# One gate of the modulation, computed in the second layer's token selection instead of in the first mixer

## The chip, the cores and the metric

One core of a Trainium2 chip runs the kernel. The metric is the device time of one execution in microseconds (us); lower is better. Five engines work beside one another, each through its own list of instructions in order: PE (TensorE, matrix products), DVE (VectorE), ACT (ScalarE), POOL (GpSimd) and SP (SyncE, here only an issuer of transfers). Sixteen DMA engines move data; they are fed by a hardware queue (transfers that SP issues) and a software queue (transfers that POOL issues).

## What is computed

A transformer of two layers for 512 image tokens ("l") and 256 context tokens ("c"), width 1024, in float32. In each layer a modulation vector of six parts is made from the condition `c`:

```python
mod_l = (silu_c @ w_mod[l] + b_mod[l])[:, None, :]
sh1, sc1, g1, sh2, sc2, g2 = jnp.split(mod_l, 6, axis=-1)
h_l = modulate(rms_norm(x, norm1_g[l]), sh1, sc1)
x = x + g1 * token_mixer(h_l, ...)
h_l = modulate(rms_norm(x, norm2_g[l]), sh2, sc2)
x = x + g2 * expert_choice_ffn(h_l, ...)
```

Each part has 1024 columns. `expert_choice_ffn` lets each of 16 experts choose its 64 best tokens (a softmax over experts, then a top-64 over tokens), runs a gated FFN of width 1024 on them, and adds the result back, times the gate `g2`. Scale 2 (`sc2`) is thus first needed where the router of a layer is prepared, gate 2 (`g2`) only where the first pair of experts has finished.

## The kernel before, in words

The program runs layer 0 and then layer 1, each in four stages: the **mixer** (input projections, retention, attention), the **output projection**, the **selection** (normalisation, router, top-64, slots) and the **experts** in eight pairs. Experts of both layers stream their weights (2 MB a load, SP's queue) through a ring of slots in on-chip memory; a load starts when the slot's last reader on PE is done.

*Modulation.* `mod_gen` (L185 to L209) makes blocks of 2048 columns. For each of eight row blocks of `w_mod` (128 rows each) it loads 2 x 512 KB on SP's queue (L197, tiles `wm`), multiplies with the 32 columns of `cT` in four matmuls that stand side by side in four column groups of PE (L201, `ps_mod`), and adds the result to `modt` on DVE (L203). One such visit is one `yield`. Block 2 holds scale 2 and gate 2. At its end the block is written to a scratch tensor in device memory (L207), and `mod_cols` (L240 to L259) transposes it with four PE transposes (L244, `ps_mc`) into the columns `A2`. The visits are woven into the first layer's projections: `m0` (L1572) is a chain of generators, `weave` takes a step of it for every so many steps of the projections and of attention, and what is left is drained when attention ends. The first layer thus computes all three blocks of the second layer as well.

*The second layer's gate.* `gates2` (L1068) reads gate 2 back, spread over 128 partitions, by one transfer on SP's queue (L264, `mod_row`); it is called in `passes` (L1748) before the last part of the selection.

*The second layer's selection.* `passes` ends with an iterator of the steps that are left (`R.fin`: the rest of `Norm2.half`, `softmax`, `keep`, `top`, `slots_l`), and the code after it opens the last three ring slots, issues their loads (`ring.load(N2)`, SP L1495) and drains the steps (L1801). On PE that is: transposes of x (L911), router products (L923), `ps_r<-qsum` (L942), four products that turn the affinities (L988, L990), then nothing until the eight rounds of top-8 on DVE are done (L996 to L999), then the products of `slots_l` (L1012, L1026). The gather of the first pair follows at once (L1111, DVE L1115, PE L1123 `ps_x`), and then its gate matrix (L1133 `ps_g`). POOL has the additions of the residual (L891) and one memset (L983) there.

The order on each engine is the order in which the tile framework's scheduler put the instructions; for the experts' stage PE's order is that of the code.

## Time and profile before

| | |
|---|---|
| median of 3 runs | 1892.11 us (1891.56 to 1894.91) |
| the profiled execution | 1889.7 us |
| its span, first to last instruction | 1887.9 us |
| mean granted clock of PE | 0.976 of 2.4 GHz |
| PE busy | 1770.4 us (94%) |
| hardware queue (SP) | 511.24 MB |
| software queue (POOL) | 15.26 MB |

Times in the rows are microseconds from the span's start. The first mixer lies at about 30 to 412, the first layer's experts end at about 1050, the second mixer at about 1330, its selection lies at 1377 to 1404, and the second layer's experts fill the time from there to 1875. A line number is that of the kernel before (L201) unless the text says "of the change". The records of PE show two rows for one float32 product, so eight records are four matmuls.

### The profile page before, as it was taken

How to read it: one execution, taken by the hardware profiler on the slowest of the kernel's cores; microseconds unless marked ns; L12 is line 12 of the kernel's file. 1: busy time of each engine (PE TensorE's matmuls, PEld its weight loads, DVE VectorE, ACT ScalarE, POOL GpSimd, SP SyncE). 2: the span in 40 equal slices, each digit the busy share in tenths (PEclk: the TensorE clock that was granted, in tenths of full speed). 3: DMA queues.
4: the chain of work that ended last, by engine and by line, in shares of the span. 5: the costliest groups of instructions: out<-in, count | busy, mean ns of one | idle time of the engine just before them, and what ended most of it. 6: DMA issues, size and time to landing. Idle time of an engine off the chain costs nothing. (4 is left out here: it accounts for less than half of the span.)

```text
span 1887.9 us, 30047 instructions
## 1 busy us (share of the span) xinstructions
PE 1770.4 (94%) x12581; PEld 1018.5 (54%) x12581; DVE 655.8 (35%) x1671; ACT 479.8 (25%) x960; POOL 329.9 (17%) x341
## 2 busy tenths in 40 slices
PE   5899999999899999999999789899959999999995
PEld 2788877767533333333333688877745444534442
DVE  5645435673621001110001755446341122221224
ACT  3435434353411001010000446454331000000001
POOL 3323123333201011011001333322410000000001
PEclk9999999999899999999999899999979999999998
DMA  8454354257789999999998411111747999999995
GB/s 278 155 191 157 106 202 151 90 186 279 300 340 408 414 401 401 423 400 399 395 412 325 169 43 37 57 34 38 297 185 291 420 430 429 429 429 428 431 428 206
DMA packets 88919, 528.42 MB, mean 280 GB/s; under 512 B 9352, under 2 KB 31932, under 8 KB 64720
## 3 DMA queue, kind: packets, MB, share of 16 engines
q1 hardware_dynamic: 83040, 511.24, 68.0%
q0 software_dynamic: 5744, 15.26, 2.9%
q8 instruction: 99, 1.62, 0.3%
q14 instruction: 36, 0.29, 0.0%
HBM read 510.41 MB, written 16.06 MB: 279 GB/s over the span
## 5 line engine op out<-in xcount | busy, mean ns | idle before, releaser
L1133 PE MATMUL ps_g<-ring,xTl 128*32 128x512 f32 (+1 forms) x1472 | 238.0, 596 | 4.2 <-DMA ring<-in_w_gate_dram 3.0
L1133 PE MATMUL ps_u<-ring,xTl 128*32 128x512 f32 (+1 forms) x1536 | 233.1, 592 | 3.1 <-DMA ring<-in_w_up_dram 2.4
L1133 PE MATMUL ps_d<-ring,aT 128*32 128x512 f32 (+1 forms) x1536 | 234.6, 593 | 0.3 <-ACT sil L1241 0.3
L1270 ACT ACTIVATE aT<-ps_t 128x512 f32<-128x512 f32 x16 | 9.6, 598 | 619.0 <-PE ps_t L1266 578.1
L354 PE MATMUL acc<-wH,hHl 128*128 128x256 f32 x512 | 153.8, 301 | 2.7 <-ACT hHl L343 1.2
L1133 PEld LDWEIGHTS ps_g<-ring,xTl 128*32 128x32 f32 (+1 forms) x1472 | 72.7, 121 | 154.1 <-issue 137.5
L1133 PEld LDWEIGHTS ps_u<-ring,xTl 128*32 128x32 f32 (+1 forms) x1536 | 69.9, 119 | 153.1 <-issue 146.0
L355 PE MATMUL acc<-wH,hLl 128*128 128x256 f32 x512 | 147.0, 287 | 3.5 <-DVE hLl L344 3.4
L356 PE MATMUL acc<-wL,hHl 128*128 128x256 f32 x512 | 147.1, 287 | 1.1 <-DVE wL L276 1.1
L1133 PEld LDWEIGHTS ps_d<-ring,aT 128*32 128x32 f32 (+1 forms) x1536 | 70.4, 119 | 142.5 <-issue 136.7
L354 PEld LDWEIGHTS acc<-wH,hHl 128*128 128x128 f32 x512 | 99.7, 195 | 30.3 <-issue 23.7
L276 POOL TENSOR_TENSOR wL<-wraw,wH 128x512 fp32r<-128x512 f32 x44 | 57.5, 1308 | 275.0 <-ACT wH L275 263.8
L355 PEld LDWEIGHTS acc<-wH,hLl 128*128 128x128 f32 x512 | 99.8, 195 | 4.4 <-DVE hLl L344 4.4
L356 PEld LDWEIGHTS acc<-wL,hHl 128*128 128x128 f32 x512 | 99.8, 195 | 4.0 <-DVE wL L276 2.4
L1268 DVE COPY aT<-ps_t 128x512 f32<-128x512 f32 x16 | 11.1, 692 | 253.2 <-PE ps_t L1266 253.2
L1249 DVE TENSOR_TENSOR sil<-ps_u,sil 128x512 f32<-128x512 f32 x32 | 22.1, 692 | 220.8 <-PE ps_u L1133 220.8
L1185 POOL TENSOR_TENSOR x<-z,xTl 128x512 f32<-128x512 f32 x3 | 5.1, 1717 | 493.4 <-DVE x L1187 493.4
L678 DVE TENSOR_REDUCE mc<-ps_s 128x1 f32<-128x513 f32 (+2 forms) x80 | 55.2, 690 | 83.3 <-PE ps_s L675 52.1
L275 ACT ACTIVATE wH<-wraw 128x512 fp32r<-128x512 f32 x88 | 55.1, 629 | 95.6 <-PE acc L355 44.9
L680 ACT ACTIVATE P<-ps_s,mc 128x513 f32<-128x513 f32 (+2 forms) x80 | 55.1, 689 | 94.5 <-DVE mc L678 94.5
L1123 PE MATMUL ps_x<-OT,xn 128*128 128x128 f32 x512 | 67.0, 297 | 8.1 <-DVE OT L1115 8.1
L1123 PEld LDWEIGHTS ps_x<-OT,xn 128*128 128x128 f32 x512 | 65.3, 210 | 10.0 <-DVE OT L1115 8.5
(491 smaller groups left out, 3172.0 us busy)
## 6 DMA issues: line engine op xcount, KB each, us to landing
ring<-in_w_up_dram SPq DMA_DIRECT2D x62, 2048.0 KB, 16.6
ring<-in_w_gate_dram SPq DMA_DIRECT2D x61, 2048.0 KB, 13.3
ring<-in_w_down_dram SPq DMA_DIRECT2D x61, 2048.0 KB, 17.0
wm<-in_w_mod_dram SPq DMA_DIRECT2D x96, 512.0 KB, 4.6
wraw<-in_w_in_dram SPq DMA_DIRECT2D x44, 512.0 KB, 3.9
wraw_o<-in_w_out_dram SPq DMA_DIRECT2D x24, 512.0 KB, 4.1
ring<-in_w_gate_dram SPq DMA_DIRECT2D x12, 512.0 KB, 4.8
ring<-in_w_down_dram SPq DMA_DIRECT2D x12, 512.0 KB, 15.6
```

Of the source, the lines that this page charges most:

```text
L275: ACT.activation(H, src, AF.Copy)
L276: sub_eng().tensor_sub(L, src, f32(H))
L354: PE.matmul(ps, aH, bH, start=start, stop=False)
L355: PE.matmul(ps, aL, bH, start=False, stop=False)
L356: PE.matmul(ps, aH, bL, start=False, stop=stop)
L678: DVE.tensor_reduce(mc[:, 0:1], sc, AX.X, OP.max, negate=True)
L680: ACT.activation(P[:, :nk + 1], sc, AF.Exp, bias=mc[:, 0:1], accum_out=mc[:, 1:2])
L1123: PE.matmul(ps[:, j], R.xn[:, t, c0:c0 + 128], OT[:, t], start=(t == 0), stop=(t == 3))
L1133: PE.matmul(G[h][c:c + n], lhs[:, k, c:c + n], W[e][:, j, 512 * h:512 * h + 512], start=(k == 0), stop=(k == KC - 1), tile_position=(0, c))
L1249: DVE.tensor_mul(sil[p][:, hs], U[h], sil[p][:, hs])
L1268: DVE.tensor_copy(aT[p][:, 4 * h:4 * h + 4], ps)
L1270: ACT.activation(aT[p][:, 4 * h:4 * h + 4], ps, AF.Copy)
```

## The change

Block 2 of the second layer is no longer made by `mod_gen`. Its two halves go separate ways.

- **Scale 2** is made in the first mixer by `mod_a2`, at the end of the same chain: only columns 4096 to 5119, so 8 loads of 512 KB instead of 16, and four visits instead of eight, each with two row blocks in the four column groups. At its end come the same four transposes, a copy, an addition of the two partial sums, and the two instructions that make `A2`.
- **Gate 2** is made in the second layer's selection by `mod_g2`: 16 loads of 256 KB on POOL's queue into three slots (`wg2`), one matmul of 32 x 512 after each, into one PSUM bank, two DVE additions of 1 x 512, two writes to the scratch tensor on SP's queue, and then `gates2`, which has moved behind all this.

```diff
+NG2 = 3
...
+    def mod_a2(wp, pp):
...
+        for k in range(0, KC, 2):
+            ps = pp.tile([128, 512], F32, name="ps_mod", tag="t", bufs=4)
+            for i in range(2):
+                w = wp.tile([128, 2, 512], F32, name="wm", tag="wraw", bufs=NW)
+                SP.dma_start(w, w_mod[1, 128 * (k + i):128 * (k + i) + 128, 4096:5120].rearrange("p (q n) -> p q n", q=2))
+                for q in range(2):
+                    g = 32 * (2 * i + q)
+                    PE.matmul(ps[g:g + 32], cT[:, k + i, :], w[:, q, :], start=True, stop=True, tile_position=(0, g))
+            DVE.tensor_add(m, m, ps)
+            if k < KC - 2:
+                yield
...
+    def mod_g2(wp, pp):
+
+        m = wp.tile([64, 512], F32, name="modg")
+        for q in range(2):
+            POOL.dma_start(m[32 * q:32 * q + 1], b_mod[1:2, 5120 + 512 * q:5632 + 512 * q])
+        ps = pp.tile([128, 512], F32, name="ps_g2", tag="acc", bufs=4)
+        for k in range(KC):
+            for q in range(2):
+                w = wp.tile([128, 512], F32, name="wg2", tag="wg2", bufs=NG2)
+                POOL.dma_start(w, w_mod[1, 128 * k:128 * k + 128, 5120 + 512 * q:5632 + 512 * q])
+                PE.matmul(ps[32 * q:32 * q + 32], cT[:, k, :], w, start=k == 0, stop=k == KC - 1,
+                          tile_position=(0, 32 * q))
+            yield
+        for q in range(2):
+            o = slice(32 * q, 32 * q + 1)
+            DVE.tensor_add(m[o], m[o], ps[o])
+            SP.dma_start(mod_d[1][2][0:1, 1024 + 512 * q:1536 + 512 * q], m[o])
...
-                    m0 = chain(mod_gen(0, wq, pp, range(1, 3)), router_cols(0, streams, pp, R), mod_gen(1, wq, pp, range(0, 3)))
+                    m0 = chain(mod_gen(0, wq, pp, range(1, 3)), router_cols(0, streams, pp, R), mod_gen(1, wq, pp, range(0, 2)), mod_a2(wq, pp))
...
-                    gates2(l, ra[0], R, two)
                     if two:
+                        gates2(l, ra[0], R, two)
...
+                if not two:
+                    with ExitStack() as s4:
+                        g2 = mod_g2(s4.enter_context(tc.tile_pool(name="g2w", bufs=1, side="right")), pp)
+                        for i, _ in enumerate(R.fin):
+                            if i >= 8:
+                                next(g2, None)
+                        drain(g2)
+                        gates2(l, ra[0], R, two)
                 drain(R.fin)
```

What the scheduler makes of it, at three places. In the listings a name like `wg_12184` is a tile with its number; lines of the change are those of the diff's new file (L280 is the matmul of `mod_g2`, L279 its load, L274 its load of `b_mod`; L942 has become L990, L990 and L988 have become L1038 and L1036, L1012 is L1060, L1026 is L1074, L1111 is L1159).

PE in the second layer's selection, before, from the router's last products to the gather:

```order
4363 L923 MATMUL ps_lg<-hsc,wrAl 32x128 x8
4364 L942 MATMUL ps_r<-qsum,lgs 128x16 x4
4365 L990 MATMUL ps_r<-ident,aff_l 16x128 x2
4366 L988 MATMUL ps_r<-ident,aff_l 16x128 x2
4367 L1012 MATMUL ps_r<-val,ident 16x64
4368 L1012 MATMUL ps_r<-fi,ident 16x64
4369 L1026 MATMUL ps_r<-ident,tok_l 64x8 x2
4371 L1111 MATMUL ps_t<-tok_l,ident 128x64 x2
```

The same place now (left out are the matmuls that only repeat, the fifth to the eleventh of sixteen):

```order
4355 L971 MATMUL ps_lg<-hsc,wrAl 32x128 x8
4356 L280 MATMUL ps_g_12183<-wg_12184,cT 32x512
4357 L990 MATMUL ps_r<-qsum,lgs 128x16 x4
4358 L280 MATMUL ps_g_12183<-wg_12187,cT 32x512
4359 L280 MATMUL ps_g_12183<-wg_12190,cT 32x512
4360 L1038 MATMUL ps_r<-ident,aff_l 16x128
4361 L280 MATMUL ps_g_12183<-wg_12193,cT 32x512
4362 L1038 MATMUL ps_r<-ident,aff_l 16x128
4363 L1036 MATMUL ps_r<-ident,aff_l 16x128 x2
4371 L280 MATMUL ps_g_12183<-wg_12246,cT 32x512
4372 L1060 MATMUL ps_r<-val,ident 16x64
4379 L280 MATMUL ps_g_12183<-wg_12264,cT 32x512
```

The sixteen matmuls of the gate stand between the selection's own: one before the router's sums, three before the affinities are turned, twelve before the result of the top-64, all sixteen before the gather.

POOL from the last additions of the residual on, now (before, its two additions L891 stood next to each other, and nothing but the memset followed):

```order
240 L939 TENSOR_TENSOR x<-x,ty 128x512
241 L274 DMA modg<-in_b_mod_dram 1x16x32 x2
242 L939 TENSOR_TENSOR x<-x,ty 128x512
243 L279 DMA wg_12184<-in_w_mod_dram 128x512
244 L279 DMA wg_12187<-in_w_mod_dram 128x512
245 L279 DMA wg_12190<-in_w_mod_dram 128x512
246 L1031 MEMSET affT 48x256
247 L279 DMA wg_12193<-in_w_mod_dram 128x512
```

Three loads are issued behind the last addition; the fourth, and each one after it, waits for the matmul that frees its slot.

PE at the end of the first mixer, before (attention's score products left out between the two groups):

```order
1956 L711 MATMUL ps_o<-PT,avl 64x256 x2
1957 L201 MATMUL ps_mod<-wm,cT 32x512 x4
1964 L711 MATMUL ps_o<-PT,avl 64x256 x4
1965 L698 MATMUL ps_t<-ident,P 128x128 x4
1966 L201 MATMUL ps_mod<-wm,cT 32x512 x4
1967 L698 MATMUL ps_t<-ident,P 128x128 x2
1968 L244 MATMUL ps_mc<-ident,modt 128x128
1969 L698 MATMUL ps_t<-ident,P 128x128 x2
1970 L244 MATMUL ps_mc<-ident,modt 128x128 x3
1971 L698 MATMUL ps_t<-ident,P 128x128 x8
```

And now:

```order
1955 L759 MATMUL ps_o<-PT,avl 64x256 x5
1962 L759 MATMUL ps_o<-PT,avl 64x256
1963 L746 MATMUL ps_t<-ident,P 128x128 x16
1964 L759 MATMUL ps_o<-PT,avc 64x256 x4
```

The last four visits are gone, two of them from this place and two from some 70 rows ahead of it, and the four transposes have moved some 90 rows ahead.

## Rows read from the trace of the kernel before

**Rows 1.** Stretches: us, busy time (instructions) by engine, granted clock, DMA share, GB/s.
```profile
360.00:400.00 40.00, 39.41 (x272) 28.83 (x272) 28.15 (x91) 15.52 (x29) 13.69 (x15) 1.00 0.36 119
400.00:412.00 12.00, 11.36 (x90) 6.77 (x88) 6.40 (x16) 7.97 (x17) 2.40 (x3) 1.00 0.50 176
1460.00:1860.00 400.00, 387.33 (x1940) 178.69 (x1938) 87.17 (x161) 31.00 (x60) 0.00 (x0) 0.99 1.00 426
```

**Rows 2.** Timeline of PE, end of the first mixer: start, length, engine, line, operation.
```profile
388.06 1.06 PE L201 MATMUL ps_mod<-wm,cT 128*32 128x512 f32 x8
389.06 0.50 PE L354 MATMUL acc<-hHl,wH 128*128 128x512 f32 x1
...
406.12 1.07 PE L201 MATMUL ps_mod<-wm,cT 128*32 128x512 f32 x8
...
408.07 0.36 PE L244 MATMUL ps_mc<-ident,modt 128*128 128x128 f32 x1 [0.51 <-ACT P L685]
```

**Rows 3.** Timeline of PE, the second layer's selection and its first gather.
```profile
1383.72 1.06 PE L942 MATMUL ps_r<-qsum,lgs 128*128 128x16 f32 x8 [0.72 <-ACT lgs L939]
1388.12 0.59 PE L990 MATMUL ps_r<-ident,aff_l 128*16 128x128 f32 x2 [3.34 <-DVE aff_l L951]
...
1400.06 0.37 PE L1012 MATMUL ps_r<-val,ident 16*16 16x64 f32 x2 [9.75 <-DVE val L996]
...
1403.34 1.08 PE L1111 MATMUL ps_t<-tok_l,ident 16*128 16x64 f32 x4 [0.43 <-DVE slot_l L1037]
1404.96 5.81 PE L1123 MATMUL ps_x<-OT,xn 128*128 128x128 f32 x32 [0.54 <-DVE OT L1115]
1411.37 7.09 PE L1133 MATMUL ps_g<-ring,xTl 128*64 128x512 f32 x32 [0.60 <-ACT xTl L1089]
1418.39 3.84 PE L1123 MATMUL ps_x<-OT,xn 128*128 128x128 f32 x32
```

**Rows 4.** Timeline of DVE: the first of the eight rounds of top-8.
```profile
1390.80 0.42 DVE L996 MAX8 val<-affT 48x8 f32<-48x256 f32 x1
```

**Rows 5.** Stretches (columns as in rows 1) around the selection, and one early.
```profile
32.00:36.00 4.00, 2.45 (x12) 1.09 (x11) 4.00 (x6) 2.84 (x6) 2.65 (x3) 1.00 0.92 306
1392.00:1396.00 4.00, 0.00 (x0) 0.00 (x0) 3.90 (x17) 1.26 (x1) 0.00 (x0) 0.50 0.37 156
1404.00:1408.00 4.00, 3.46 (x16) 3.31 (x17) 1.13 (x4) 0.00 (x0) 0.00 (x0) 0.50 1.02 344
```

**Rows 6.** Timeline of POOL and of SP's transfers, start of the selection.
```profile
1376.40 3.44 POOL L891 TENSOR_TENSOR x<-x,ty 128x512 f32<-128x512 f32 x2 [3.02 <-DVE ty L890]
1377.03 0.80 SPq L1495 DMA_DIRECT2D ring<-in_w_up_dram  x2
```

**Rows 7.** DMA queues, 1380 to 1393: packets, MB, share of the 16 DMA engines.
```profile
q1 hardware_dynamic: 370, 5.54, 99.7%
```

**Rows 8.** Line L192, b_mod loads of 8 KB on POOL's queue: ns of an issue, landing.
```profile
L192 POOL DMA_DIRECT2D modt<-in_b_mod_dram x10: 549/564/573, 31.3 to 260.8; - x10
...
DMA to landing us min/median/max: 2.1/3.6/5.8
```

**Rows 9.** Tile xe, 1000 to 1040: three loads of 1 MB on POOL's queue, beside the ring.
```profile
DMA to landing us min/median/max: 11.4/12.3/13.1
```

**Rows 10.** DMA queues, 1021 to 1022: those loads (rows of 4 KB) beside the ring.
```profile
q1 hardware_dynamic: 20, 0.33, 76.4%
q0 software_dynamic: 23, 0.09, 22.9%
```

**Rows 11.** DMA queues, 616 to 617: POOL's scatter (rows of 2 KB) beside the ring.
```profile
q1 hardware_dynamic: 19, 0.31, 74.1%
q0 software_dynamic: 18, 0.03, 18.8%
```

**Rows 12.** Timeline of SP's transfers: the first ring loads that need a slot freed by the experts.
```profile
1413.33 16.88 SPq L1501 DMA_DIRECT2D ring<-in_w_gate_dram  x12
```

**Rows 13.** Tile g, five broadcasts of a gate (512 KB, L264): time to landing.
```profile
DMA to landing us min/median/max: 7.1/10.7/14.3
```

More of the change, by code (lines that the diff above doesn't have):

```diff
@@ L238, in mod_half @@
             DVE.scalar_tensor_tensor(A1[0][r][:, cs], tmp[:, 1, :, r], 1.0, n1col[0][:, cs], op0=OP.add, op1=OP.mult)
+        yield
+    def mod_a2(wp, pp):
+        m = wp.tile([128, 512], F32, name="modt", tag="modt", bufs=2)
+        POOL.memset(m, 0.0)
+        for r in range(2):
+            POOL.dma_start(m[r:64:32], b_mod[1, 4096:5120].rearrange("(q n) -> q n", q=2))
+        for k in range(0, KC, 2):
[9 more added lines that the diff above has]
+                yield
+        ps = pp.tile([128, 4, 4, 32], F32, name="ps_mc", tag="t", bufs=4)
+        for j in range(4):
+            PE.transpose(ps[:, j].rearrange("p q r -> p (q r)"), m[:, j::4], ident)
+        tmp = m[:, 0:32].rearrange("p (q s r) -> p q s r", q=4, r=2)
+        DVE.tensor_copy(tmp, ps[:, :, :, 0:2].rearrange("p s q r -> p q s r"))
+        DVE.tensor_tensor(tmp[:, 0:2], tmp[:, 0:2], tmp[:, 2:4], OP.add)
+        for r in range(2):
+            DVE.scalar_tensor_tensor(A2[1][r].rearrange("p (q s) -> p q s", q=2), tmp[:, 0:2, :, r], 1.0,
+                                     n2col[1].rearrange("p (q s) -> p q s", q=2), op0=OP.add, op1=OP.mult)
+        yield
@@ new lines, in mod_g2 @@
+    def mod_g2(wp, pp):
[9 more added lines that the diff above has]
+                          tile_position=(0, 32 * q))
+            yield
+        for q in range(2):
+            o = slice(32 * q, 32 * q + 1)
+            DVE.tensor_add(m[o], m[o], ps[o])
+            SP.dma_start(mod_d[1][2][0:1, 1024 + 512 * q:1536 + 512 * q], m[o])
```

## The prediction

> **What bounds the kernel now.** I read the page's forty slices first, to find the stages, then stretches of a few microseconds in the two stages that the change touches, then their timelines. In the first mixer PE sets the pace: from 360 to 400 it is busy 39.4 of 40 us at the full 2.4 GHz clock [rows 1], so work taken off PE there comes off the time. The last 12 us are less tight (11.36 of 12). In the experts the transfers set the pace: from 1460 to 1860 the DMA engines are busy 1.00 of the time at 426 GB/s, PE 387 of 400 [rows 1]. The stream that fills this time is limited by slots: its first transfer that waits for the experts starts at 1413.33 [rows 12], 2 us after the first gate matmul at 1411.37 [rows 3]. What makes the selection longer therefore moves the start of the stream, and the end, by the same amount. The selection is a chain: router sums on PE at 1383.72, affinities turned from 1388.12, the top-64 on DVE from 1390.80, its result on PE at 1400.06, the gather's first matmul (L1111) at 1403.34 [rows 3, 4]. PE is idle in most of it, and that is the room which the change uses. But PE takes its instructions in order, so a matmul that waits for its load holds up those behind it.
>
> **What the mixer gains.** Eight visits of four matmuls become four. A visit starts at 388.06 and the next product at 389.06 [rows 2]: 1.00 us. The four that go are the last four, 388.06 to 406.12. Three of them stand among work that PE does without a gap: 3.0 us. The fourth and the four transposes (408.07) stand where PE waits for ACT's softmax (0.51 us, released by ACT P) [rows 2], so ACT is late next and I count 0.3 us of a possible 1.5. Half of the 16 loads of 512 KB on SP go too; the DMA share there is 0.36 [rows 1], so that is worth nothing. Four DVE additions go, and a few small ones come, under PE's cover. Together -3.3 us, bounds -2 and -4.5.
>
> **What the selection loses.** The first load of gate 2 is issued on POOL behind the last residual addition, which ends at 1376.40 + 3.44 = 1379.84 [rows 6], and behind the two loads of b_mod, 0.56 us each [rows 8]: 1380.9. The second addition itself is moved back by those 1.1 us, into a gap in front of the last transposes, where PE was still at the products ahead of them; I count nothing.
>
> How long does such a load take? Alone, an 8 KB load on this queue lands in 2.1 us at best [rows 8]; 256 KB at 426 GB/s add 0.6: 2.7 us, the lower bound. But three ring loads are issued from 1377.03 [rows 6] and fill the DMA engines until about 1393.5 (share 0.997 up to 1393, 0.37 from 1392 to 1396) [rows 5, 7]. Where both queues have work, the rows show piece against piece: in one microsecond 20 ring pieces of 16 KB and 23 of 4 KB from POOL's queue [rows 10], and 19 against 18 where POOL moves rows of 2 KB [rows 11]. A load of this change is 128 rows of 2 KB, 8 for each of 16 engines. A ring piece takes 16 KB x 16 / 426 GB/s = 0.62 us of its engine, so eight turns of 0.62 + 0.08 are 5.6 us, and the first load lands near 1380.9 + 2.1 + 5.6 = 1388.6. As an upper bound, 1 MB loads beside the ring took 11.4 us and more [rows 9]; with half as many pieces an engine, 7.7 us fits between.
>
> The Trainium skill ("DMA: Bandwidth & Descriptors", section Queues, rings and completion order) states that an engine turns between queues by whole packets, typically of 9 to 17 descriptors. By that rule the eight rows of a load would go in one turn and the first would land near 1384; rows 10 and 11 speak for turns of single pieces, and I go by them. The rule's outcome is the first rival.
>
> Now the chain. A matmul of 32 x 512 is two records; the gate rows show 32 records in 7.09 us, two side by side [rows 3], so one alone takes 7.09 / 16 x 2 = 0.88 us, at half clock 1.77. PE has been waiting since 1383 and its clock falls to 0.50 when it idles, as in rows 5. So the first gate matmul ends at 1390.4, and the router sums start there instead of at 1383.72: +6.7. The affinities take 4.4 us more [rows 3], to 1394.8; the second and third load, which PE needs before it turns them, land 5.6 us later (1394.2) and soon after, when the ring is through; the fourth, issued when the first slot came free at 1390.4, lands about 1396.2 and stands between the two transposes. With their matmuls at half clock the second transpose comes near 1399, and the top-64 starts 2.4 us behind it, at 1401 instead of 1390.8: +10. It lasts 9.7 us, to 1411.
>
> The remaining twelve loads run three at a time. A slot's round is 0.6 issue, 2.7 to land and 0.9 for the matmul: 4.2 us, or 1.4 a load. The fifth lands near 1400, the sixteenth at 1400 + 11 x 1.4 = 1415.4, and its matmul ends at 1416.3. L1111 stands behind it: +13 against 1403.34. If the issue lies within the 2.7 the round is 3.6 us, and it is +11. I take **+12**; the bounds are +1 (each load in 2.7 us from the start) and +17 (the clock stays at half, 5.1 us a round: 1400 + 18.7 + 1.8).
>
> **What else moves.** PE is then no longer idle ahead of the gather. Before, its clock stood at 0.50 from 1392 to 1396 and still from 1404 to 1408, and the gather's 32 records took 5.81 us; the next 32 took 3.84 [rows 3, 5]. Early in the program PE kept the full clock while busy 2.45 of 4 us [rows 5], and the gate's matmuls make it about that busy. So -2.0 us, bounds 0 and -2.5. The two DVE additions of one row stand ahead of the gather's one-hot (L1115), which waits for L1111 anyway: +0.4, bounds 0 and 1.4. On SP the two writes and the broadcast of the gate now stand behind the selection, ahead of the slot-bound ring loads. The additions (1 us) and a write of a few KB (2.1 to 5.8 us, as the loads of rows 8) after the sixteenth matmul let SP go on 3 to 7 us later, and those ring loads are due 10 us after L1111 [rows 3, 12], 8 with the faster gather: covered. The broadcast lands in 7.1 to 14.3 us [rows 13], and its first reader, the end of the first pair, comes some 70 us on. If that cover went, SP's delay would add to the stream one to one.
>
> **Sum.** -3.3 + 12 + 0.4 - 2.0 = **+7.1 us**. The profiled execution took 1889.7 us (span 1887.9), which gives 1896.8; the median shown is 2.4 above it, so against the median I forecast **1899.2 us**. About 0.2% (3.8 us) is what a measurement can tell from no change.
>
> **Rivals.**
> - *The loads come early.* A load's eight pieces pass the ring pieces in one turn; the first lands by 1384, and rounds of 3.6 to 4.2 us bring the sixteenth by 1404 to 1405. The selection loses 1 to 2 us, the mixer and the gather give 5.3: -3 to -5, 1887 to 1889, not slower than before. It decides at a landing of about 3.3 us: with rounds much longer than that the sixteen no longer fit into 1381 to 1403. For it: from 1394 on the DMA engines are free. Against: rows 10 and 11. Chance 0.22. The Trainium skill's rule above speaks for this one.
> - *Two rows a turn.* Pieces of 2 KB go in pairs, as 4 KB rows did in rows 10: the first load lands at 1385.7, the top-64 starts 6 us late, the end of the loads is at +7: net +2, 1894. Chance 0.16.
> - *PE stays at half clock* through the loads: selection +17, gather no faster: +14, 1906. For it: 0.50 at PE idle [rows 5]. Against: at 1.77 us a matmul, with a round of 5.1 us for three, PE would hardly idle. Chance 0.13.
> - *The change doesn't lighten the mixer*: the four visits filled gaps that the softmax leaves, and nothing comes off; +10, 1902. Against: 39.4 of 40 us busy. Chance 0.05.
>
> **Chances.** The forecast has the remaining 0.44, with its own range of +3.5 to +10. Faster by over 0.2% is most of the first rival and a little of the second: 0.20. Within 0.2%: the rest of these and the forecast's lower edge: 0.21. Slower: 0.59. The range is to leave out the edge of the first rival and of the cold one: 1887.5 to 1906.
>
> **What would show it.** Right: in the changed profile PE's idle time ahead of the router sums and of the transposes ends with the landing of `wg2`; the first `wg2` lands 6 us or more after its issue, the later ones in about 3; the sixteenth matmul ends after 1410 on a clock set back by 3 us; the gather's 32 records take below 4.5 us. The mixer ends 3 us earlier. Wrong: `wg2` loads land in 3 us from the first on, the top-64 starts within 2 us of before, or the gather is reached before the mixer's gain is spent.

## The result, and the profile after

The change takes 1908.59 us (median of 4 runs, 1908.42 to 1917.79) against 1891.84 us (median of 4 runs of the kernel before on the same chip): a ratio of 1.0104, 95% interval 1.0083 to 1.0125. It is slower, by more than twice the forecast, and above the range. The profiled execution took 1908.42 us, its span 1906.6.

The timeline of PE in the second layer's selection, in the kernel of the change (start, length, line, operation, count; in brackets the idle time before it and what ended it). L280 is the gate's matmul, L990 the router's sums, L1038 and L1036 the turned affinities, L1060 the result of the top-64, L1159 the first product on the chosen slots, L1171 the gather, L1181 the experts' first product; the last product of the output projection starts at 1371.47:

```profile
1371.47 0.39 PE L404 MATMUL acc<-wL,mHl 128*128 128x512 f32 x1
...
1377.25 0.43 PE L971 MATMUL ps_lg<-hsc,wrAl 128*32 128x128 f32 x8 [0.28 <-DVE hsc L962]
1384.78 1.91 PE L280 MATMUL ps_g<-wg,cT 128*32 128x512 f32 x2 [7.10 <-DMA wg<-in_w_mod_dram]
1386.62 1.89 PE L990 MATMUL ps_r<-qsum,lgs 128*128 128x16 f32 x8
1388.44 1.92 PE L280 MATMUL ps_g<-wg,cT 128*32 128x512 f32 x2
1391.67 1.91 PE L280 MATMUL ps_g<-wg,cT 128*32 128x512 f32 x2 [1.31 <-DMA wg<-in_w_mod_dram]
1393.51 0.38 PE L1038 MATMUL ps_r<-ident,aff_l 128*16 128x128 f32 x1
1393.83 1.92 PE L280 MATMUL ps_g<-wg,cT 128*32 128x512 f32 x2
...
1396.63 0.39 PE L1036 MATMUL ps_r<-ident,aff_l 128*16 128x128 f32 x1 [0.57 <-DVE affT L1039]
...
1408.60 0.28 PE L1060 MATMUL ps_r<-val,ident 16*16 16x64 f32 x2
...
1413.73 1.04 PE L280 MATMUL ps_g<-wg,cT 128*32 128x512 f32 x2
1416.35 0.62 PE L1159 MATMUL ps_t<-tok_l,ident 16*128 16x64 f32 x4 [1.57 <-DVE modg L285]
1421.49 5.15 PE L1171 MATMUL ps_x<-OT,xn 128*128 128x128 f32 x32 [4.52 <-DVE OT L1163]
1427.24 7.09 PE L1181 MATMUL ps_g<-ring,xTl 128*64 128x512 f32 x32 [0.60 <-ACT xTl L1137]
```

The same product of the output projection in the profile before:

```profile
1376.56 0.39 PE L356 MATMUL acc<-wL,mHl 128*128 128x512 f32 x1
```

From the last out-projection product to the first gate product [rows 3] it was 34.8 us; it is 55.8 now, +21.0. Three places hold it: 7.10 us ahead of the first gate matmul, with the router's sums behind it; the matmuls and waits ahead of the affinities and up to L1159; and, not in the forecast at all, 4.52 us ahead of the gather. What stands behind that last one is in the timelines of DVE (one-hot OT, L1163) and of SP's transfers in the same kernel:

```profile
1414.82 1.39 DVE L285 TENSOR_TENSOR modg<-modg,ps_g 1x512 f32<-1x512 f32 x2 [0.92 <-PE ps_g L280]
1421.04 1.13 DVE L1163 TENSOR_SCALAR OT<-ps_t,tokc 128x128 f32<-128x128 f32 x4 [4.84 <-DMA mod<-modg]
```

```profile
1415.52 0.95 SPq L286 DMA_DIRECT2D mod<-modg  x2
1420.98 0.34 SPq L312 DMA_DIRECT2D g<-mod  x1
1429.20 5.96 SPq L1549 DMA_DIRECT2D ring<-in_w_gate_dram  x8
```

The slot-bound ring loads start at 1429.20, 15.9 us later than at 1413.33 [rows 12], and 1.96 us behind the first gate product as before.

The span is 18.7 us longer than before's. It adds up from four pieces: this execution reaches the last out-projection product 5.1 us earlier; the selection takes 21.0 more; from the first gate product to the last matmul it is 459.7 us instead of 458.1; and from the last matmul to the end 19.7 instead of 18.5. Most of the 5.1 is no gain of the change: from 1060 to 1100, in the second mixer, the granted clock of this execution was 1.00, of the profile before 0.90, and of the kernel without the gate (below) 0.89; that kernel has the change's first mixer and reaches the product at 1377.43. So all comparisons below count from the last out-projection product, and the verdicts from the timed runs.

### The profile page after: what moved, and what is told of

Same layout as the page of the kernel before. It is cut to its first block, busy times and chain, and to the rows that moved or that the text cites. A ratio compares the mean times of both kernels' runs of the same rounds, so it can differ in the third digit from the quotient of the medians.

```text
span 1906.6 us, 30070 instructions
## 1 busy us (share of the span) xinstructions
PE 1786.5 (94%) x12581; PEld 1018.6 (53%) x12581; DVE 655.8 (34%) x1671; ACT 480.2 (25%) x960; POOL 338.3 (18%) x357
## 5 line engine op out<-in xcount | busy, mean ns | idle before, releaser
L1181 PE MATMUL ps_g<-ring,xTl 128*32 128x512 f32 (+1 forms) x1472 | 235.7, 593 | 4.1 <-DMA ring<-in_w_gate_dram 2.9
L1181 PE MATMUL ps_u<-ring,xTl 128*32 128x512 f32 (+1 forms) x1536 | 234.8, 595 | 3.1 <-DMA ring<-in_w_up_dram 2.4
L1181 PE MATMUL ps_d<-ring,aT 128*32 128x512 f32 (+1 forms) x1536 | 233.5, 593 | 0.3 <-ACT sil L1289 0.3
L1181 PEld LDWEIGHTS ps_g<-ring,xTl 128*32 128x32 f32 (+1 forms) x1472 | 72.0, 121 | 152.4 <-issue 136.5
L1181 PEld LDWEIGHTS ps_u<-ring,xTl 128*32 128x32 f32 (+1 forms) x1536 | 70.3, 119 | 154.4 <-issue 147.3
L1181 PEld LDWEIGHTS ps_d<-ring,aT 128*32 128x32 f32 (+1 forms) x1536 | 70.1, 119 | 141.6 <-issue 137.1
L1171 PE MATMUL ps_x<-OT,xn 128*128 128x128 f32 x512 | 68.0, 300 | 12.1 <-DVE OT L1163 12.1
L1171 PEld LDWEIGHTS ps_x<-OT,xn 128*128 128x128 f32 x512 | 66.4, 213 | 14.0 <-DVE OT L1163 8.6
```

What stands on the lines that cost most here:

```text
L1171: PE.matmul(ps[:, j], R.xn[:, t, c0:c0 + 128], OT[:, t], start=(t == 0), stop=(t == 3))
L1181: PE.matmul(G[h][c:c + n], lhs[:, k, c:c + n], W[e][:, j, 512 * h:512 * h + 512], start=(k == 0), stop=(k == KC - 1), tile_position=(0, c))
```

## The experiments

My theory: what costs is that PE, which takes its instructions in order, waits for the gate's loads, which are slow beside the ring at first and three at a time later. Rivals: the matmuls' own time; POOL's path; a wait for the memory of the gate's row; the mixer gaining nothing.

All versions in one table. The four middle columns are us from the start of the last out-projection product to the router's sums, to the last pair of turned affinities, to the product on the slots, and to the first gate product of the experts; "end" is from the start of the last matmul to the end of the span.

```
version            sums  affin.  slots   gate    end   ratio  (95% interval)
before              7.2   12.7   26.8   34.8   18.5
no_gate             7.2   12.7   26.8   34.7   18.3   0.9985 (0.9974 to 0.9997)
the change         15.2   25.2   44.9   55.8   19.7   1.0104 (1.0083 to 1.0125)
eight_visits       14.0   25.1   44.5   55.6   19.9   1.0111 (1.0097 to 1.0126)
gate_read_early    15.1   25.1   44.7   55.8   19.7   1.0098 (1.0078 to 1.0119)
modg_own           18.9   26.1   44.1   51.9   19.7   1.0076 (1.0060 to 1.0093)
slots8             15.4   26.4   41.4   48.9   19.7   1.0079 (1.0062 to 1.0096)
two_loads          15.2   23.5   38.4   47.3   18.6   1.0057 (1.0039 to 1.0076)
late8               6.9   12.8   35.4   42.3   19.8   1.0048 (1.0030 to 1.0067)
ring_behind         8.8   15.9   34.4   41.6   19.7   1.0038 (1.0024 to 1.0052)
pool_alone16       10.1   14.5   29.5   37.8   19.8   1.0007 (0.9996 to 1.0019)
early16             7.2   12.8   28.1   37.0   18.4   0.9995 (0.9984 to 1.0006)
early16_adds_late   7.2   12.7   28.0   36.9   18.4   1.0012 (1.0002 to 1.0023)
early16_auto        8.2   12.7   27.7   35.2   18.5   1.0007 (0.9995 to 1.0018)
```

**The mixer alone** (no_gate). The block of `mod_g2` is gone, and the old read stands in its place:

```diff
-        mod_row(R.g2, l, 2, 1024, 0)
+        mod_row(R.g2, l, 2 if two else 1, 1024, 0)
...
+                    gates2(l, ra[0], R, two)
                     if two:
-                        gates2(l, ra[0], R, two)
...
-                if not two:
-                    with ExitStack() as s4:
...
```

> Gate 2 of the second layer is not computed at all (the gate is read from another block of the modulation, in its old place); scale 2 keeps its four visits. What is left of the change is what the mixer gains. My theory: the mixer gains 2 to 3.3 us and the selection is that of before: 34 to 36 us from the last product of the output projection to the first gate product of the experts, against 34.81 before and 55.77 in the change; time 1888.5 to 1890, ratio 0.998 to 0.999. Rival, the visits filled gaps that the softmax leaves: ratio 1.000, and the stretch from the last product of the first ps_mc group to the first out-projection product is as long as before. Second rival, the four-visit form costs something itself: over 1.001.

0.9985, which is 2.8 us with an interval from 0.6 to 4.9, and the selection of before to 0.1 us. So computing the gate in the selection carries the whole loss, with what it adds behind the selection.

**The row's memory** (modg_own).

```diff
-        m = wp.tile([64, 512], F32, name="modg")
+        m = ra[0].tile([64, 512], F32, name="modg")
```

> The change, with the gate's row (modg) in memory that nothing takes over, so that the one-hot of the first gather (OT) no longer has to wait until the two writes out of that row have landed. My theory: DVE's wait of 4.84 us ahead of OT goes, PE's idle 4.5 us ahead of the gather shrinks to under 1.5, and the stretch from the last out-projection product to the first gate product is 55.8 - 3 to 5 = 51 to 53 us; ratio about 1.0075 to 1.009 against 1.0104 for the change. Rival, another wait ends right behind (the slots' values, or the copies of the PSUM bank): still 54 us or more, ratio 1.010.

51.9 us, 1.0076: as expected. Timeline of DVE in this version:

```profile
1421.97 1.13 DVE L1163 TENSOR_SCALAR OT<-ps_t,tokc 128x128 f32<-128x128 f32 x4 [0.62 <-PE ps_t L1159]
```

OT waits 0.62 us, for its product, instead of 4.84 for a transfer. In the change OT comes from a pool that is opened after the gate's pool is closed, and it waits until the two writes out of the gate's row have landed, 5.5 us after the first was issued (1415.52 to 1420.98). OT reads nothing of that row, and the wait goes when the row has memory of its own; so OT was placed over the row. No address was read. The scheduler also moved a few other things here (three gate matmuls stand ahead of the sums), so the 3.9 us are not this wait alone; from the slots to the gate product it is 7.8 us instead of 10.9, which is its part.

**Fewer loads** (two_loads).

```diff
-                w = wp.tile([128, 512], F32, name="wg2", tag="wg2", bufs=NG2)
...
+                if k == 0:
+                    ws.append(wp.tile([128, 512], F32, name="wg2", tag="wg2", bufs=NG2))
+                    POOL.dma_start(ws[q], w_mod[1, 128 * k:128 * k + 128, 5120 + 512 * q:5632 + 512 * q])
+                PE.matmul(ps[32 * q:32 * q + 32], cT[:, k, :], ws[q], start=k == 0, stop=k == KC - 1,
```

> The change, with only the first two of the gate's sixteen loads; the sixteen matmuls all read these two tiles (left out: fourteen loads, so the gate's values are others). PE does the same matmuls in the same order. My theory (loads are what is waited for): only the wait for the first load is left, about 7 us ahead of the router's sums; the rounds of three go, and L1159 comes 30 to 36 us behind the last out-projection product instead of 44.9 (26.8 before); stretch to the first gate product 43 to 47 us instead of 55.8, ratio 1.004 to 1.006. Rival (the matmuls' own time on PE, 16 of 1 to 1.9 us, is what it costs): L1159 still at 41 us or more, stretch over 51 us, ratio 1.008 or more.

Between the two theories: 38.4 us to the slots, 6.5 less than in the change, 2.4 more than I allowed. The first landing keeps the sums at 15.2; behind it the matmuls' own time is a cost too, since six matmuls (12 records) take 5.30 us between the sums and the affinities, the records at up to 1.06 us, and affinities that stood 5.6 us behind the sums now stand 8.3. The first landing accounts for 8.0 us of the 18.1 up to the slots (sums at 15.2 instead of 7.2), the fourteen other loads for the 6.5, and the matmuls ahead of the affinities for 2.7 (8.3 - 5.6), in which half-clock records and their mere number are not told apart.

**The ring behind the gate** (ring_behind).

```diff
-                    ring.more(r2_s.enter_context(tc.tile_pool(name=f"rb{l}", bufs=1, side="right")), N2)
-                    ring.load(N2)
...
                         gates2(l, ra[0], R, two)
+                    ring.more(r2_s.enter_context(tc.tile_pool(name=f"rb{l}", bufs=1, side="right")), N2)
+                    ring.load(N2)
```

> The change, with the ring's three loads of the selection issued behind the gate's loads instead of ahead of them, so that the gate's loads have the DMA engines to themselves. My theory (the first landing is long because its pieces take turns with the ring's 16 KB pieces): the first load lands within 3.5 us of its issue instead of about 9.6, the router's sums start 5 to 7 us earlier than in the change, and the stretch to the first gate product is 47 to 51 us instead of 55.8; the rounds of the later loads stay at 3 to 4.5 us. Time: the gain less what the ring's late loads take from the experts, ratio 1.006 to 1.010. Rival (POOL's own path is slow to start, whatever the ring does): the first landing is 7 us or more, the stretch 54 us or more, ratio 1.010 or worse.

This is the largest single step: 41.6 us, 1.0038, better than I expected on both counts. Not all of it is the loads. Up to the slots it is 34.4 us, 10.5 less than in the change; the other 3.7 lie between the slots and the gate product (7.2 us instead of 10.9), since OT no longer waits for the row here, although the row has no memory of its own. Timeline of DVE in this version:

```profile
1404.89 1.13 DVE L1163 TENSOR_SCALAR OT<-ps_t,tokc 128x128 f32<-128x128 f32 x4 [0.81 <-PE ps_t L1159]
```

By the order of the code the ring's slots are opened behind the gate's pool here, ahead of OT's; that it is they that lie over the row is not shown. The tile `wg` in the change and then in this version, DMA to landing:

```profile
DMA to landing us min/median/max: 2.9/3.2/15.3
```

```profile
DMA to landing us min/median/max: 3.0/3.1/3.9
```

The long landings are gone with the ring's pieces, so POOL's path is not slow in itself. What the two queues did in the change while both were moving data, the DMA queues from 1379.5 to 1381.5 (packets, MB, share of the engines; q8 has one packet more):

```profile
DMA packets 80, 0.82 MB, mean 410 GB/s; under 512 B 0, under 2 KB 0, under 8 KB 40
q1 hardware_dynamic: 39, 0.64, 75.2%
q0 software_dynamic: 40, 0.16, 20.8%
```

39 pieces of the ring (16 KB) to 40 of the gate: turns of single pieces, one to one, as in [rows 10, 11]. But a piece of the gate is 4 KB here, two of the load's rows of 2 KB, so a load is four turns of each engine and not eight. By the packets of the trace the first load, issued at 1375.19, has its first piece at 1379.06, 3.9 us later, when of the two loads of `b_mod` ahead of it in POOL's queue the first has just landed and the second has not (6.1 and 6.5 us after their issue). Fifteen of its sixteen completion writes start from 1382.11 to 1383.02, about four turns on, and the last engine's only at 1384.29: 9.5 us from issue to landing. What holds the first piece and that one engine back, no run settles.

**Slots** (slots8): `NG2 = 3` becomes `NG2 = 8`.

> The change with eight slots (NG2) for the gate's loads instead of three. My theory (rounds of three loads, each waiting for a matmul to free its slot): the first landing stays long (8 us or more, as it is the ring's pieces that it takes turns with), so the router's sums start as late as in the change, 14 to 17 us behind the last out-projection product; but the loads behind it no longer wait for matmuls, so L1159 comes 37 to 42 us behind the last out-projection product instead of 44.9, and the time falls by 3 to 7 us, ratio 1.0065 to 1.009. Rival (all the loss is the first landing and PE's order, the rounds are hidden by the top-64): L1159 at 44 us or more, ratio 1.010. The wait of OT for the write of the gate's row stays.

41.4 us to the slots and 1.0079, as expected. One thing was not: the wait of OT is gone too (7.6 us from the slots to the gate product). The gate is finished before the top-64 ends, its writes are issued at 1412.23, and nothing waits for them any more.

**PE's order by hand** (late8): eight slots, the row's own memory, and

```diff
-                        for i, _ in enumerate(R.fin):
-                            if i >= 8:
-                                next(g2, None)
-                        drain(g2)
+                        for _ in range(8):
+                            next(R.fin)
+                        with tc.manual_schedule(engines={mybir.EngineType.PE}):
+                            for _ in range(3):
+                                next(R.fin)
+                            for _ in R.fin:
+                                next(g2, None)
+                            drain(g2)
```

> Eight slots, the gate's row in memory of its own, and PE's order written out by hand from the router's sums on: all sixteen gate matmuls stand behind the turned affinities, in the room of the top-64; the loads still stand behind the last residual addition on POOL, beside the ring. My theory (what costs is that PE waits for loads ahead of the router's sums and of the affinities): router's sums 7 to 8 us behind the last out-projection product as before the change (15.1 in the change), the first top-8 round where it was before (14 us behind it, 25 in the change), and only the tail of the loads is left: L1159 at 28 to 35 us instead of 44.9 (26.8 before), ratio 1.000 to 1.004. Rival (the ring's pieces hold all sixteen loads back whatever PE's order is): L1159 at 38 us or more, ratio 1.006 or more.

The first half is as expected: the sums are at 6.9 and the affinities at 12.8, as before the change. But the loads land up to 17.9 us after their issue, and the sixteenth matmul still ends behind the top-64: 35.4 to the slots and 1.0048, just above what I expected. PE's order moves the wait; it does not remove it.

**Loads early** (early16): all sixteen loads on SP's queue ahead of the ring's, sixteen slots, the third ring slot opened when these are free, the row's own memory, PE's order as in late8.

```diff
-NG2 = 3
+NG2 = 16
...
+        for k in range(KC):
+            for q in range(2):
+                ws.append(wp.tile([128, 512], F32, name="wg2", tag="wg2", bufs=NG2))
+                SP.dma_start(ws[-1], w_mod[1, 128 * k:128 * k + 128, 5120 + 512 * q:5632 + 512 * q])
+        yield
...
-                    ring.more(r2_s.enter_context(tc.tile_pool(name=f"rb{l}", bufs=1, side="right")), N2)
-                    ring.load(N2)
+                    ring.more(r2_s.enter_context(tc.tile_pool(name=f"rb{l}", bufs=1, side="right")), N2 - 1)
...
+                        next(g2)
+                        ring.load(N2 - 1)
...
+                    ring.more(r2_s.enter_context(tc.tile_pool(name=f"rc{l}", bufs=1, side="right")), 1)
+                    ring.load()
```

> A version meant to hide the gate: all sixteen loads on SP's queue ahead of the ring's loads, into sixteen slots (the third ring load of the selection comes when these are free again), the gate's row in memory of its own, all sixteen matmuls behind the turned affinities. My theory: every load has landed before the affinities are turned, the matmuls (9 to 14 us) lie in the 9.75 us in which PE waited for the top-64, L1159 comes 26 to 29 us behind the last out-projection product (26.8 before), the gather's 32 records take under 5 us instead of 5.8, and the mixer's 2.8 us are kept: ratio 0.998 to 1.000. Rival (the ring's loads, late by 7 to 25 us, are missed in the experts): stretch to the first gate product as before, but the experts longer by 3 us or more, ratio 1.000 to 1.003. Second rival, the matmuls at half clock overrun the top-64: L1159 at 32 us or more, ratio over 1.001.

0.9995: the loss is gone, and it cannot be told from the kernel before. The matmuls fit into the room of the top-64. The gather did not get warmer, though: 6.68 us instead of under 5. PE was done early and idle again for 2.66 us, and the granted clock, 1.00 from 1396 to 1400, was 0.66 in the next 4 us and 0.50 from 1404 to 1408. The idle time alone does not set the gather's time: behind 7.42 us of it early16_auto (below) shows 5.38 us; no run settles what does. And the two additions of the row on DVE stood in the chain of the top-64's result, where PE waited 1.18 us for it.

**The same, two details** (early16_adds_late, early16_auto). In the first DVE's order is written out too, and the last two gate matmuls stand behind the L1060 pair; in the second only PE's order goes back to the scheduler's.

> early16 with DVE's order written out too: the two additions of the gate's row (0.68 us each) behind the slots instead of in the chain of the top-64's result, and the last two gate matmuls behind the first products of that result. In early16 L1159 (there L1163) came 28.1 us behind the last out-projection product (26.8 without the gate), 1.2 us of it PE waiting for DVE between the two L1064. My theory: that wait goes, the product of the slots stands at 26.8 to 27.5 us, the first gate product at 35 to 36.5 (37.0 in early16, 34.7 without the gate), ratio 0.9985 to 0.9995. Rival (the additions only move into OT's way, or PE's clock at the gather decides): first gate product at 37 us or more, ratio 0.9995 to 1.000.

> early16 with PE's order left to the scheduler, as in the change: five gate matmuls ahead of the router's sums, eight ahead of the turned affinities. Only PE's order differs from early16. My theory (in-order PE): the loads land 5 to 7.5 us after their issue at 0.5 us behind the last out-projection product, so the router's products and sums wait for them a little and for the matmuls: sums at 9 to 12 us instead of 7.2, affinities at 16 to 20 instead of 12.8, L1159 at 31 to 34 instead of 28.1, ratio 1.0005 to 1.003. Rival (with early loads PE's order no longer matters): L1159 within 1.5 us of early16, ratio as early16 (0.9995).

Neither met my theory. In the first the gate product, 36.9, is just under the rival's 37, and the ratio, 1.0012, lies above both ranges. In the second the profile is the rival's (L1159 0.5 us from early16's); the ratio, 1.0007, fits either. With the additions behind the slots, L1159 (there L1165) waits for them instead. Timeline of PE, early16_adds_late:

```profile
1404.50 1.08 PE L1165 MATMUL ps_t<-tok_l,ident 16*128 16x64 f32 x4 [1.73 <-DVE modg L289]
```

As in the change (1.57 there, released by DVE's `modg` L285), L1159 stands behind the additions, which are not free in either place. That it is the PSUM bank they read which holds it up is likely, but another bank for the gate was not tried.

With early loads the scheduler's order costs nothing in the selection: slots at 27.7 and gate product at 35.2, against 28.1 and 37.0 with my own order. The times don't show it as better: the 1.8 us are lost again between the first gate product and the last matmul (460.6 us against 458.8). Stretches of early16_auto and then of the change (us, busy time by engine, granted clock, DMA share, GB/s):

```profile
1380.00:1384.00 4.00, 4.00 (x38) 1.84 (x36) 2.50 (x14) 1.78 (x4) 0.30 (x1) 1.00 0.93 313
1384.00:1388.00 4.00, 3.39 (x18) 1.45 (x16) 1.99 (x10) 3.43 (x3) 0.00 (x0) 1.00 1.05 386
```

```profile
1380.00:1384.00 4.00, 0.00 (x0) 0.00 (x0) 0.00 (x0) 1.83 (x1) 0.00 (x0) 0.50 1.04 438
1392.00:1396.00 4.00, 4.00 (x6) 0.36 (x4) 0.00 (x0) 3.85 (x2) 0.54 (x1) 0.50 0.40 117
1396.00:1400.00 4.00, 3.43 (x11) 1.02 (x10) 2.61 (x10) 0.00 (x0) 1.41 (x3) 0.50 0.23 77
1400.00:1404.00 4.00, 2.74 (x6) 0.28 (x4) 3.90 (x17) 0.00 (x0) 1.27 (x3) 0.95 0.64 197
```

In early16_auto the granted clock stays at the full 2.4 GHz through all sixteen matmuls (1.00 up to 1396), and the longest record of one is 0.617 us; it is 0.50 from 1400 on, after PE has waited 7.42 us for the top-64. In the change PE was idle from 1380 to 1384, the clock fell to half, and it was still there from 1392 to 1400, with PE busy for 4.00 and 3.43 of 4 us: the gate matmuls there ran at up to 1.06 us a record. The wait costs twice, once itself and once in what follows.

**The queue** (pool_alone16): ring_behind with sixteen slots and the row's own memory.

> The change with sixteen slots, the gate's row in memory of its own, and the ring's three loads behind the gate's: as early16_auto, but the sixteen loads go through POOL's queue, behind the last residual addition, and have the DMA engines to themselves. It tells two things apart. First, the end of the program: in the six versions with sixteen gate loads on POOL's queue the span ends 19.7 to 19.8 us after the start of the last matmul, in the kernel before, in those without these loads, with two of them and in the three with the loads on SP's queue 18.3 to 18.6 us; if it is the queue, it is 19.7 here, if it is the slots or the order, 18.4. Second, the selection: the loads are issued from 3.7 us behind the last out-projection product, 0.54 us apart, and land about 3 us later, the last near 16 us; so PE waits little: router's sums at 8.5 to 10.5 us, L1159 at 27.5 to 31, first gate product at 35 to 38.5 us (41.6 with three slots, 35.2 in early16_auto). Ratio 1.000 to 1.003. Rival (POOL's loads slow one another down): landing over 6 us, first gate product at 40 us or more, ratio 1.003 or more.

As expected: 37.8 us, 1.0007, and the end of the program at 19.8 us. One thing was not: the loads land in 5.1 to 5.7 us with this many in flight, instead of about 3; that much the order of the work hides.

**The broadcast of the gate** (gate_read_early) and **the mixer the other way** (eight_visits):

```diff
-        mod_row(R.g2, l, 2, 1024, 0)
+        mod_row(R.g2, l, 2 if two else 1, 1024, 0)
...
+                    gates2(l, ra[0], R, two)
                     if two:
-                        gates2(l, ra[0], R, two)
...
                         drain(g2)
-                        gates2(l, ra[0], R, two)
```

> The change, but the gate that the experts use is read from another block of the modulation, in the old place ahead of the selection (left out: the read of the freshly computed gate; it is still computed and written). It measures what the 512 KB broadcast costs in its new place, beside the experts' stream. From the first gate product to the end of the span the change takes 479.4 us, the kernel before 476.5, the one without gate 476.6. My theory, the broadcast takes its 1.2 us of DMA time (512 KB at 426 GB/s) out of the stream: 477.5 to 478.5 here, time 1 to 2 us below the change's, ratio 1.0095 to 1.010. Rival (the difference is scatter of single executions): 479 us or more, or below 477.

478.2 us, in the range I gave, but other versions that have the broadcast in its new place lie at 477.2 to 480.3: one execution doesn't show it. The ratio, 1.0098, doesn't tell it from the change either. Inconclusive.

```diff
-                    m0 = chain(mod_gen(0, wq, pp, range(1, 3)), router_cols(0, streams, pp, R), mod_gen(1, wq, pp, range(0, 2)), mod_a2(wq, pp))
+                    m0 = chain(mod_gen(0, wq, pp, range(1, 3)), router_cols(0, streams, pp, R), mod_gen(1, wq, pp, range(0, 3)))
```

> The change, but the first mixer makes scale 2 and gate 2 in eight visits as before (gate 2 is thus computed twice; the selection's one is used). What it is above the change is what the mixer gains. In the profiles so far, from the first product of the context's second projection (hHc,wH, at 273 to 277 us) to the first out-projection product it is 139.6 us before and 137.5 to 138.4 in eleven versions with four visits: 1.7 us. My theory now: 139 to 140 us here, time 1 to 2.5 us above the change's, ratio 1.0105 to 1.012. Rival (the forecast's 3.3 us were right): 2.5 to 4.5 us above, ratio 1.012 to 1.013. Rival (no gain at all): 1.0104 again, 138 us here.

1.0111 and 139.9 us, against 138.0 in the change: 1.9 us in the profile, 1.3 in the ratio, within what I expected the second time. The intervals of the two ratios overlap, though, so the times don't tell it from no gain; the profiles do. The two timelines' rows for that stretch in the change, its first and last:

```profile
275.18 0.39 PE L402 MATMUL acc<-hHc,wH 128*128 128x256 f32 x1
413.19 1.19 PE L402 MATMUL acc<-wH,mHl 128*128 128x512 f32 x4 [0.99 <-ACT mHl L323]
```

and in eight_visits:

```profile
276.10 0.38 PE L402 MATMUL acc<-hHc,wH 128*128 128x256 f32 x1
416.00 1.19 PE L402 MATMUL acc<-wH,mHl 128*128 128x512 f32 x4 [1.00 <-ACT mHl L323]
```

## Why the prediction was wrong

The side was right (slower, 0.59) and so was the mechanism of the forecast case, PE waiting in order for loads beside the ring. The size was not: +7.1 was forecast, and 1.0104 is +19.7 us (15.7 to 23.6). Two terms fell short by about 5 us each: what follows the gate's additions (5.6 us for 0.4) and the loads' chain up to the sixteenth matmul (4.5 us more than its +12). By the terms of the sum:

- *The mixer, -3.3.* The stretch that holds the visits of block 2 takes 139.6 and 139.9 us in the profiles with eight visits and 137.5 to 138.4 in the twelve with four, 1.8 us between the means, so the term was too large by about half, below the bound of -2, though the timed runs of no_gate (0.6 to 4.9) do not exclude it. In both versions PE waits for ACT at the end of this stretch (1.00 and 0.99 us), which fits: work taken off PE ahead of such a wait gives back less than its own time.
- *The selection up to L1159, +12.* It is +18.1, above the upper bound of +17. The steps in order. The first load lands so that its matmul starts 13.3 us behind the last out-projection product; forecast were 12.0 (1388.6). That this came near is luck: the prediction counts eight turns of 2 KB where the trace shows four of 4 KB, and leaves out the 3.9 us ahead of the first piece and the late engine. The sums, forecast at 13.8 us, come at 15.2. The sixteenth matmul, forecast to end at 39.7, ends at 43.3 (1413.73 + 1.04 - 1371.47): the first seven matmuls ran at half clock (1.91 us alone, where 1.77 and then 0.9 were reckoned), and the last ten loads were issued 1.6 us apart instead of 1.4. Then the 1.57 us behind the additions.
- *The two additions, +0.4, "ahead of the gather's one-hot (L1115), which waits for L1111 anyway".* **This is the step that failed.** I looked at the additions' time on DVE and not at what is behind them: L1159 waits for them (1.57 us), and the row they write is read by two transfers, while its memory already belongs to OT: DVE waits 4.84 us, and PE 4.52 ahead of the gather instead of 0.54 [rows 3]. Together that is 5.6 us. The bound of 1.4 was no bound; modg_own and slots8 each take the OT wait away, and from the slots to the gate product they show 7.8 and 7.6 us instead of 10.9. It is not the whole miss: without the OT wait modg_own is still at 1.0076, 14 us above the kernel before.
- *The gather, -2.0.* Its 32 records took 5.15 us instead of 5.81 [rows 3]: 0.7 us. It was to start on a full clock, but while PE was idle for 4.52 us just ahead of it the granted clock fell from 1.00 (1412 to 1416) to 0.69 and then 0.50 (1420 to 1424).
- *SP's later issue, "covered".* Right: the ring's slot-bound loads start 1.96 us behind the gate product in both kernels.
- *Not in the sum:* 1.2 us at the end of the program (below), and 0.4 to 2.6 us more between first gate product and last matmul in the versions that compute the gate in the selection; no run settles where these come from.

The rivals. "The loads come early" is out: its landing of about 3 us is what ring_behind shows when the ring is out of the way, and 9.6 us is what two_loads measured beside the ring. The rule of the Trainium skill ("DMA: Bandwidth & Descriptors", section Queues, rings and completion order) is that an engine turns by whole packets of typically 9 to 17 descriptors; the prediction made of it that a load's eight rows go in one turn. This trace does not agree with that: 39 pieces of the ring passed to 40 of the gate, and a piece of the gate held two rows. "Two rows a turn" is thus right on the turns and wrong on the landing: it reckoned 4.8 us from issue to landing, and 9.5 were measured. "The change doesn't lighten the mixer" is out by no_gate, whose whole interval lies below 1, and by the stretch of 139.6 and 139.9 us. "PE stays at half clock" (1906) came nearest in time, and half of it holds: the clock was at half up to 1400, but came back to 0.95 and 1.00 for the last nine matmuls.

## What to carry to other kernels

Work moved into an engine's idle time costs nothing only if its operands are there before that engine reaches it: here the same sixteen matmuls cost 21 us of the selection behind three slots beside a bulk stream, and 0.4 us of it with all loads issued ahead of that stream and the row in memory of its own. Check what the moved work leaves behind as well: which tile takes over the memory of its last operand, and which transfer still reads from it. And a wait on PE was paid here a second time, in half-clock work behind it.

No version that computes the gate beats the kernel before by more than the measurement can tell; the best of those with the gate in the selection (0.9995) only gives the loss back.

## What the runs showed of the hardware that I had not expected

The end of the program depends on how many transfers POOL has issued in it, though in the change it issues the last of them at 1410. In the eight versions with sixteen gate loads on that queue the span ends 19.7 to 19.9 us after the start of the last matmul; in the six others (no gate loads, two of them, or all on SP's queue) 18.3 to 18.6. The last matmul in the change, and before:

```profile
1886.90 0.40 PE L1214 MATMUL ps_s<-yL,OH 128*128 128x512 f32 x1
```

```profile
1869.42 0.40 PE L1166 MATMUL ps_s<-yL,OH 128*128 128x512 f32 x1
```

The work between is the same instruction for instruction, and the output's transfers land a median 2.0 us after their issue in both. The 1.2 us lie in POOL's closing DRAIN, the longest of its three in the rows of the program's last line, in the change and before (ns min/median/max, first and last start):

```profile
L1958 POOLq DRAIN  x3: 51/102/9901, 1895.9 to 1906.4; - x3
```

```profile
L1902 POOLq DRAIN  x3: 51/97/8594, 1878.5 to 1887.6; - x3
```

It starts 9.0 us behind the start of the last matmul in every version, and its length goes with the number of transfers that POOL issued in the whole program: 8.44 us at 71 (no_gate), 8.59 at 73 (before and the three with early16 in their name), 8.76 at 75 (two_loads), 9.90 at 89 (the change and six others, one of them at 9.91) and 10.06 at 91 (eight_visits). That is 0.08 us a transfer. What the engine does in that time no row shows.

A load of 256 KB does not move in the same pieces on both queues. By the packets of the trace the sixteen loads are 1024 pieces of 4 KB on POOL's queue (the change) and 2048 of 2 KB on SP's (early16_auto).
